# One query tile of 128 rows for the later chunk of two heads, in three attentions of a two-layer encoder

## The chip, the cores and the metric

The kernel runs on one core of a Trainium2 chip. The metric is the device time of one execution in microseconds (us); lower is better. TensorE (PE in the profile) multiplies matrices, VectorE (DVE), ScalarE (ACT) and GpSimd (POOL) work on tiles elementwise, SyncE (SP) issues the DMA transfers. Each engine works through its own list of instructions in order and waits for the others by semaphores.

## The reference, cut to what matters

Two layers of an encoder run over 1024 frames of a first chunk group ("prompt") and over 64 frames of a later chunk ("sample"), which have 256 cached keys and their own 64. Layer 0 has two groups of 8 heads, latent attention (A) and band attention (B), layer 1 has 16 heads of stick-breaking attention (C). Head size is 64. Around them stand projections, an output projection, layer norms and an MLP with 4096 hidden features.

```python
def _softmax_attend(q, k, v, mask, scale):               # A
    s = jnp.einsum('bqhd,bkhd->bhqk', q, k).astype(jnp.float32) * scale
    p = jax.nn.softmax(jnp.where(mask, s, NEG_INF), axis=-1)
    return jnp.einsum('bhqk,bkhd->bqhd', p.astype(v.dtype), v)

def _band_sample(q, k_all, v_all, n_past, table):        # B, later chunk
    ...
    s = jnp.einsum('bqhd,bkhd->bhqk', q, k_all).astype(jnp.float32) * BAND_SCALE + bias[None]
    p = jax.nn.softmax(s, axis=-1)
    return jnp.einsum('bhqk,bkhd->bqhd', p.astype(v_all.dtype), v_all)

def _stick_breaking(q, k, v, q_pos, k_pos):              # C
    z = jnp.einsum('bqhd,bkhd->bhqk', q, k).astype(jnp.float32) * SB_SCALE
    mask = k_pos[None, :] < q_pos[:, None]
    log_1m = jnp.where(mask, jax.nn.log_sigmoid(-z), 0.0)
    tail = lax.cumsum(log_1m, axis=z.ndim - 1, reverse=True) - log_1m
    w = jnp.where(mask, jnp.exp(jax.nn.log_sigmoid(z) + tail), 0.0)
    return jnp.einsum('bhqk,bkhd->bqhd', w.astype(v.dtype), v)
```

## The kernel before, in words

**Numbers.** Everything is fp32. [...]

**Heads.** Heads go in pairs: 4 in B, then 4 in A, then 8 in C. `heads64` (L444, for B and C) makes a pair's tiles: `qH` and `qL` (128 x 2 x 1088: both heads' queries of all 1088 rows, the half that belongs to the other part filled so that one K of 128 holds a product of two parts), `kS` (the keys) and `V` (128 x 11 x 2 x 128: 11 blocks of 128 keys, the last of which has only the 64 own keys of the later chunk; the value's high and low parts lie beside each other in the columns). In A a pair's queries come by DMA into `q` (128 x 2 x 1088), one tile per head, and the keys are `k0H` and the like. Two sets of tiles take turns by the pair's parity.

**Units.** `attend` (L649) walks `self.order`, a list of (head, unit). Units 0 to 3 are two blocks of 128 queries of the first group, unit 4 is the 64 later queries, a unit of its own for each head. A unit makes its rows of weights (`row_band`, `row_mla`, `row_stick`: scores on TensorE at L522 and L523, or by `mm3` in A; then softmax, or the scan and the product of C, on DVE, ACT and POOL into the tiles `R`, `Rs` or `G`), and `weigh` (L590) then transposes the weights block by block on TensorE (L161, into the PSUM tile `t`), splits them into `wtH` and `wtL`, and multiplies them with `V` into `pv` (L634, L635). For a late unit the scores have 64 query columns as the stationary operand, the transposes have 64 rows (two of 64 x 128 and one of 64 x 64), and the value matmuls of block 10 have 64 rows on both sides:

```python
            wH = self.tl(cp, [P, 512], "wtH", 3, F32R)
            ...
                nc.tensor.matmul(out, v, wH[:nkey, s : s + n], start=first, stop=False)
                nc.tensor.matmul(out, v, wL[:nkey, s : s + n], start=False, stop=last)
```

Then the two halves of `pv` are added: ACT copies the lower half to `otmp` (L637), DVE adds (L643); in A (`pool_fold`) ACT copies both (L637, L640) and POOL adds (L641). SP stores `o` (3 buffers) into `oT_d`, or `oTl_d` for the last pair of A and of C (L646).

**Order.** A scheduler with a simulated timeline fixes the order on each engine. `paced` (L507) ties each projection step of the next pair to the mark (first transpose) of a unit of the running one, so that the projections (L143 to L145, tile `d`) lie among the attention's matmuls. With the last pair of A and of C, the first output projections (`out_early`) take this place; behind it, `out_proj` (L949) loads `oTl_d` and `oT_d` in tiles `sl` and `xs`.

Of the kernel before, what the change touches and what calls it, by code (L numbers as in the profile page):

```python
# [7 lines left out]
F32 = mybir.dt.float32  # L8
# [5 lines left out]
P = 128  # L14
# [95 lines left out]
class Net:  # L110
# [3 lines left out]
    def __init__(self, tc, io):  # L114
        self.tc, self.nc, self.io = tc, tc.nc, io
        self.uid = 0
        self.alt = False
        self.wturn = 0
        self.pool_fold = False
# [324 lines left out]
    def heads64(self, cp, bp, qp, bufs, pair, w, cacheT, cache_v, outs, out0, cache_outs=(None, None), first=None):  # L444
# [16 lines left out]
        def step(kind, c0, n):  # L461
# [17 lines left out]
            if kind == "q":  # L479
                for h in range(2):  # L480
                    r, c = half[h], slice(c0, c0 + n)
                    self.split(qH[r, h, c], qL[r, h, c], ps[r, :n])
                    nc.scalar.activation(qH[half[1 - h], h, c], ps[r, :n], AF.Copy)
                return mark
# [17 lines left out]
        heads = []  # L502
        for h in range(2):
            heads.append(([qH[:, h, :], qL[:, h, :]], [kS[:, h, :]]))
        return heads, V, steps

# [11 lines left out]
    def scores(self, qk, qc, nq, kc, n, tag="s"):  # L518
        ps = self.ps(tag)
        q, k = ([x[:, c : c + m] for x in y] for y, c, m in zip(qk, (qc, kc), (nq, n)))  # L520
        if len(k) == 1:
            self.nc.tensor.matmul(ps[:nq, :n], q[0], k[0], start=True, stop=False)  # L522
            self.nc.tensor.matmul(ps[:nq, :n], q[1], k[0], start=False, stop=True)  # L523
        else:
            self.mm3(ps[:nq, :n], *q, *k)
        return ps

    def softmax_tail(self, rp, R, nq, nk, sums):
        nc = self.nc
        inv = self.tl(rp, [P, 1], "inv", 4)  # L530
        nc.vector.reciprocal(inv[:nq], sums)  # L531
        nc.gpsimd.tensor_tensor(R[:nq, :nk], R[:nq, :nk], inv[:nq].to_broadcast([nq, nk]), op=ALU.mult)  # L532

    def row_band(self, rp, qk, bias, qc, nq, kc, nk, off):
# [4 lines left out]
        for i, (a, n) in enumerate(pcs):  # L539
            ps = self.scores(qk, qc, nq, kc + a, n)  # L540
            nc.vector.tensor_tensor_reduce(
                R[:nq, a : a + n], ps[:nq, :n], bias[:nq, off + a : off + a + n], op0=ALU.add, op1=ALU.max, scale=1.0,
                scalar=-3e38 if i == 0 else mx[:nq, 0:1], accum_out=mx[:nq, i : i + 1])
        nm = self.tl(rp, [P, 1], "nm", 4)
        nc.vector.tensor_scalar(nm[:nq], mx[:nq, len(pcs) - 1 : len(pcs)], -SCALE, None, op0=ALU.mult)
        sm = self.tl(rp, [P, 1], "sm", 4)
        nc.scalar.activation(R[:nq, :nk], R[:nq, :nk], AF.Exp, bias=nm[:nq], scale=SCALE, accum_out=sm[:nq])
        self.softmax_tail(rp, R, nq, nk, sm[:nq])
        return [(0, nk, R)]

    def row_mla(self, rp, qk, qc, nq, kc, nk):
# [4 lines left out]
        for i, (a, n) in enumerate(pcs):  # L556
            ps = self.scores(qk, qc, nq, kc + a, n, tag="ds")
            nc.vector.tensor_tensor_reduce(
                R[:nq, a : a + n], ps[:nq, :n], self.zero[:nq].to_broadcast([nq, n]), op0=ALU.add, op1=ALU.max, scale=1.0,
                scalar=-3e38 if i == 0 else mx[:nq, 0:1], accum_out=mx[:nq, i : i + 1])  # L560
        nc.vector.tensor_scalar(nm[:nq, 0:1], mx[:nq, len(pcs) - 1 : len(pcs)], -MLA_SCALE, None, op0=ALU.mult)
        nc.scalar.activation(R[:nq, :nk], R[:nq, :nk], AF.Exp, bias=nm[:nq, 0:1], scale=MLA_SCALE, accum_out=sm[:nq, 0:1])
        self.softmax_tail(rp, R, nq, nk, sm[:nq, 0:1])
        return [(0, nk, R)]

    def row_stick(self, rp, qk, qc, nq, kc, nk):
# [1025 lines left out]
```

## Time and profile before

| | us |
|---|---|
| runs timed | 2878.89, 2874.23, 2879.42; median 2878.89 |
| profiled execution | 2872.33 (its span 2870.5, mean TensorE clock 0.986) |
| busy PE | 2766.8 (96% of the span, 16955 instructions) |
| busy DVE | 2165.0 (75%) |
| busy ACT | 1525.1 (53%) |
| busy POOL | 795.9 (28%) |
| chain of waits that ended last | PE 77%, DVE 9%, DMA 6%, ACT 3% |

The span falls into stages: latents up to 140 us, attention B 140 to 410, loads and query projections for A 410 to 497, A 497 to 690, output projection and MLP 690 to 1480, C 1480 to 2080 (its last pair from 1995 on), output projection and MLP to the end. In a timeline row of TensorE the second number is the modelled duration, which overlaps with the next; what a matmul costs is read from start to start.

### The profile page before, as it was taken

The page shows a single profiled execution, that of the slowest core. Times are in us where ns is not written, and L with a number is a line of the kernel's source. Part 1 is how long each engine was busy: PE and PEld are TensorE (multiplying, and loading weights), DVE is VectorE, ACT ScalarE, POOL GpSimd, SP SyncE. Part 2 cuts the span into 40 slices and gives each one's busy share as a digit, 9 for nine tenths or more (in the row PEclk, how much of TensorE's full clock was granted, in tenths as well). Part 3 has the DMA queues.
Part 4 walks back from the last instruction along what each step waited for, and adds up shares of the span by engine and source line. Part 5 has one row for each costly group of instructions (what it writes and reads, how often), then busy time and mean ns, then how long its engine had stood idle before and what let it go on. Part 6 is the DMA issues. An engine that isn't in the chain of part 4 may idle for free.

```text
span 2870.5 us, 47260 instructions
## 1 busy us (share of the span) xinstructions
PE 2766.8 (96%) x16955; PEld 2512.4 (88%) x16955; DVE 2165.0 (75%) x3905; ACT 1525.1 (53%) x3156; POOL 795.9 (28%) x900
## 2 busy tenths in 40 slices
PE   7999988999999999999999999999999999999998
PEld 7999977887899998888789999998779999977786
DVE  4256674785877777899987888888677777789998
ACT  4266653883455555433247777777444555553331
POOL 2123340662300002222533444444330000122235
PEclk9999999999999999999999999999899999999999
DMA  7222246334334447444231111112142344654432
GB/s 228 59 65 58 58 134 166 83 96 124 114 113 159 138 147 256 140 156 129 88 111 54 51 58 54 51 50 100 49 162 100 128 161 135 211 188 140 158 119 77
DMA packets 232041, 334.96 MB, mean 117 GB/s; under 512 B 43296, under 2 KB 165440, under 8 KB 230784
## 3 DMA queue, kind: packets, MB, share of 16 engines
q1 hardware_dynamic: 231808, 331.95, 36.5%
q8 instruction: 134, 2.20, 0.3%
q14 instruction: 99, 0.81, 0.1%
HBM read 217.18 MB, written 113.33 MB: 115 GB/s over the span
## 4 chain that ended last, share of the span: by engine, by line
PE 77%; DVE 9%; DMA 6%; ACT 3%; issue 3%; POOL 1%; SPq 1%; DVEq 0%; ACTq 0%; POOLq 0%
PE d L143 9%; PE d L145 9%; PE d L144 9%; PE s L143 5%; PE s L145 5%; PE s L144 5%; PE t L143 5%; PE t L145 5%; PE t L144 5%; PE t L161 5%; PE pv L634 3%; PE pv L635 2%; PE pv L145 2%; PE pv L143 2%; PE pv L144 2%
## 5 line engine op out<-in xcount | busy, mean ns | idle before, releaser
L585 POOL TENSOR_TENSOR G<-G,S 128x384 f32<-128x384 f32 (+4 forms) x208 | 210.3, 1013 | 330.5 <-DVE S L582 139.4
L143 PE MATMUL d<-xH,wH 128*128 128x384 f32 (+1 forms) x792 | 265.6, 335 | 3.7 <-ACT kraw L493 3.5
L145 PE MATMUL d<-xH,wL 128*128 128x384 f32 (+1 forms) x792 | 264.0, 333 | 1.6 <-DVE wL L139 1.6
L144 PE MATMUL d<-xL,wH 128*128 128x384 f32 (+1 forms) x792 | 263.9, 333 | 0.0
L139 DVE TENSOR_TENSOR wtL<-t,wtH 128x512 fp32r<-128x512 f32 (+4 forms) x376 | 200.8, 556 | 45.4 <-ACT wtH L138 42.7
L138 ACT ACTIVATE wtH<-t 128x512 fp32r<-128x512 f32 (+4 forms) x376 | 175.9, 497 | 75.1 <-PE t L161 42.1
L634 PE MATMUL pv<-wtH,V 128*128 128x256 f32 (+3 forms) x720 | 189.4, 285 | 11.7 <-DVE o L643 4.2
L532 POOL TENSOR_TENSOR R<-R,inv 128x640 f32<-128x640 f32 (+6 forms) x104 | 125.3, 1215 | 252.0 <-DVE inv L531 114.2
L635 PE MATMUL pv<-wtL,V 128*128 128x256 f32 (+3 forms) x720 | 183.6, 292 | 5.3 <-DVE wtL L139 5.3
L582 DVE TENSOR_TENSOR_SCAN S<-S,own 128x129 f32<-128x129 f32 (+2 forms) x144 | 150.0, 1047 | 20.0 <-ACT S L576 18.1
L634 PEld LDWEIGHTS pv<-wtH,V 128*128 128x128 f32 (+1 forms) x720 | 140.8, 196 | 27.2 <-ACT o L640 6.7
L143 PEld LDWEIGHTS d<-xH,wH 128*128 128x128 f32 x792 | 149.3, 189 | 7.7 <-ACT kraw L493 5.5
L145 PEld LDWEIGHTS d<-xH,wL 128*128 128x128 f32 x792 | 149.2, 188 | 3.5 <-DVE wL L139 1.9
L144 PEld LDWEIGHTS d<-xL,wH 128*128 128x128 f32 x792 | 149.4, 189 | 2.1
L635 PEld LDWEIGHTS pv<-wtL,V 128*128 128x128 f32 (+1 forms) x720 | 140.8, 196 | 9.1 <-DVE wtL L139 7.7
L138 ACT ACTIVATE wo<-wo 128x1024 fp32r<-128x1024 f32 (+4 forms) x100 | 88.0, 883 | 111.7 <-DMA wo<-a_d 20.3
L522 PE MATMUL s<-kS,qH 128*128 128x384 f32 (+4 forms) x312 | 114.8, 370 | 9.6 <-ACT G L577 6.2
L161 PE MATMUL t<-ident,G 128*128 128x128 f32 (+2 forms) x624 | 111.4, 279 | 6.0 <-POOL S L574 4.4
L576 ACT ACTIVATE S<-s 128x384 f32<-128x384 f32 (+4 forms) x208 | 101.8, 490 | 17.7 <-PE s L523 15.8
L523 PE MATMUL s<-kS,qL 128*128 128x384 f32 (+4 forms) x312 | 105.0, 338 | 0.0
L139 DVE TENSOR_TENSOR wo<-wo,wo 128x1024 fp32r<-128x1024 f32 (+3 forms) x72 | 83.8, 1164 | 26.4 <-ACT wo L138 26.3
L577 ACT ACTIVATE G<-s 128x384 f32<-128x384 f32 (+4 forms) x208 | 102.2, 492 | 0.8 <-PE t L161 0.8
(1702 smaller groups left out, 9778.2 us busy)
## 6 DMA issues: line engine op xcount, KB each, us to landing
wo<-a_d SPq DMA_DIRECT2D x53, 512.0 KB, 5.1
a_d<-wo SPq DMA_DIRECT2D x34, 544.0 KB, 4.4
sl<-a_d SPq DMA_DIRECT2D x29, 512.0 KB, 3.5
wo<-in_w_up SPq DMA_DIRECT2D x26, 512.0 KB, 3.9
wo<-in_w_dn SPq DMA_DIRECT2D x25, 512.0 KB, 5.9
sl<-in_w_dn SPq DMA_DIRECT2D x23, 512.0 KB, 4.9
xs<-a_d SPq DMA_DIRECT2D x19, 512.0 KB
a_d<-sl SPq DMA_DIRECT2D x17, 544.0 KB, 3.8
```

The source lines that it names most:

```text
L138: self.nc.scalar.activation(H, src, AF.Copy)
L139: (engine or self.nc.vector).tensor_tensor(L, src, H.bitcast(F32), op=ALU.subtract)
L143: i = mm(out, aH, bH, start=first, stop=False)
L144: mm(out, aH, bL, start=False, stop=False)
L145: mm(out, aL, bH, start=False, stop=last)
L161: return self.nc.tensor.transpose(out, in_, self.ident[:n, :n])
L522: self.nc.tensor.matmul(ps[:nq, :n], q[0], k[0], start=True, stop=False)
L532: nc.gpsimd.tensor_tensor(R[:nq, :nk], R[:nq, :nk], inv[:nq].to_broadcast([nq, nk]), op=ALU.mult)
L582: nc.vector.tensor_tensor_scan(s, s, own, carry, op0=ALU.mult, op1=ALU.max)
L585: nc.gpsimd.tensor_tensor(G[:nq, :n], G[:nq, :n], S[:nq, 1 : n + 1], op=ALU.mult)
L634: nc.tensor.matmul(out, v, wH[:nkey, s : s + n], start=first, stop=False)
L635: nc.tensor.matmul(out, v, wL[:nkey, s : s + n], start=False, stop=last)
```

## The change

The later queries of both heads of a pair become one unit of 128 rows. `self.order` has 9 entries instead of 10; (0, 4) now stands for both heads, and the last (1, 4) is gone. The queries stand in a tile `qS`, head 0 in columns 0 to 63 and head 1 in 64 to 127, zeros elsewhere, so that two accumulated products (one per head) give the 128 rows of scores. The last block of keys is filled up: rows 64 to 127 of `V`'s block 10 are zeroed once, and `pad` zeroes the last 64 columns of the weights. `set64` makes one set of tiles per parity for a whole attention, with the zeros written once, where `heads64` made tiles and zeros for each pair. In A, `q` holds only the first group's queries and `qS` is zeroed by POOL and loaded by 4 small DMAs per pair. In B the biases of both late heads are loaded into `blate`. `weigh` is left with full blocks, and `weigh_late` is new; `otmp` is used in A alone, elsewhere ACT copies into `o` and DVE adds there.

```diff
-        self.order = [(0, 3), (1, 0), (0, 2), (1, 1), (0, 4), (1, 3), (0, 0), (1, 2), (0, 1), (1, 4)]
+        self.order = [(0, 3), (1, 0), (0, 2), (1, 1), (0, 4), (1, 3), (0, 0), (1, 2), (0, 1)]
...
+    def set64(self, qp):
+        qH, qL = (self.tl(qp, [P, 2, SEQ], f"q{x}", 1, F32R) for x in "HL")
+        qS = self.tl(qp, [P, 2, 2, P], "qS", 1, F32R)
...
+        for h in range(2):
+            zero(qL[half[1 - h], h, :])
+        zero(qS)
+        zero(V[DEC:, 10])
...
+                    if m < n:
+                        c = slice(h * DEC, h * DEC + DEC)
+                        self.split(qS[r, h, 0, c], qS[r, h, 1, c], ps[r, m:n])
+                        nc.scalar.activation(qS[half[1 - h], h, 0, c], ps[r, m:n], AF.Copy)
...
+    def pad(self, R, nk):
+        n = -(-nk // P) * P
+        if n > nk:
+            self.nc.gpsimd.memset(R[:, nk:n], 0.0)
+        return n
...
+    def turn_weights(self, cp, blocks):
+        tp = self.ps("t")
+        mark = None
+        for i, (x, c) in enumerate(blocks):
+            t = self.transpose(tp[:, i * P : i * P + P], x[:, c : c + P])
...
+    def put_output(self, cp, pv, width):
+        nc = self.nc
+        o = self.tl(cp, [64, 256], "o", 3)
+        if self.pool_fold:
+            tmp = self.tl(self.pool_fold, [64, 256], "otmp", 2)
...
+        else:
+            nc.scalar.activation(o[:, :width], pv[64:128, :width], AF.Copy)
+            nc.vector.tensor_tensor(o[:, :width], pv[:64, :width], o[:, :width], op=ALU.add)
...
+    def weigh_late(self, cp, R, heads):
+        mm = self.nc.tensor.matmul
+        pv = self.ps("pv", (P, 256))
+        wH, wL, mark = self.turn_weights(cp, [(R[0][2], j * P) for j in range(3)])
+        for h, (V, hh, _) in enumerate(heads):
+            out = pv[:, h * DEC : h * DEC + DEC]
+            for j in range(3):
+                s = slice(j * P + h * DEC, j * P + h * DEC + DEC)
+                mm(out, V[:, 8 + j, hh, :], wH[:, s], start=j == 0, stop=False)
+                mm(out, V[:, 8 + j, hh, :], wL[:, s], start=False, stop=j == 2)
+        o = self.put_output(cp, pv, P)
...
+            qS = self.tl(mp, [P, 2, 2, P], "qS", 2, F32R)
+            nc.gpsimd.memset(qS.bitcast(F32), 0.0)
```

The order on TensorE in attention C, one late unit: `s` are scores, `t` transposes, `d` projections of the next pair, `pv` the outputs. Before, head 0 of a pair:

```order
L523 MATMUL s_18112<-kS_17742,qL_17741 128x512
L161 MATMUL t_17716<-ident_58,G_17706 64x64
L145 MATMUL d_18699<-xH_3484_16259,wL_4001_18689 128x384
...
L145 MATMUL d_18731<-xH_3483_16258,wL_4001_18689 128x384
L634 MATMUL pv_17715<-wtH_17718,V_16804 128x64
L635 MATMUL pv_17715<-wtL_17719,V_16804 128x64
L634 MATMUL pv_17715<-wtH_17727,V_16804 128x64
L635 MATMUL pv_17715<-wtL_17728,V_16804 128x64
```

and with the change (a pair):

```order
L542 MATMUL s_18143<-kS_16550,qL_16548 128x512
L161 MATMUL t_18079<-ident_58,G_18065 128x128 x3
L674 MATMUL pv_18021<-wtH_18027,V_16551 128x256
...
L143 MATMUL d_18549<-xH_3306_16007,wH_3782_18482 128x320
L691 MATMUL pv_18078<-wtH_18083,V_16551 128x64
L692 MATMUL pv_18078<-wtL_18084,V_16551 128x64
...
L692 MATMUL pv_18078<-wtL_18084,V_16551 128x64
L542 MATMUL s_18173<-kS_16550,qH_16547 128x512
```

The transpose of 64 x 64 and the two value matmuls on the 64-row block are gone; three transposes of 128 x 128 stand together, and the value matmuls, six per head, lie in one run without a block of its own shape in it.

The order on GpSimd where attention A begins: `R` and `Rs` are weights that it scales by `inv`. Before:

```order
L532 TENSOR_TENSOR R_5894<-R_5894,inv_5910 128x1024
L532 TENSOR_TENSOR Rs_5971<-Rs_5971,inv_5982 128x128
L532 TENSOR_TENSOR Rs_5985<-Rs_5985,inv_5996 128x256
L532 TENSOR_TENSOR R_6018<-R_6018,inv_6034 128x640
L532 TENSOR_TENSOR R_6037<-R_6037,inv_6053 128x768
```

and with the change:

```order
L880 MEMSET qS_5700 128x512
L880 MEMSET qS_6368 128x512
L549 TENSOR_TENSOR R_5745<-R_5745,inv_5761 128x896
L549 TENSOR_TENSOR R_5764<-R_5764,inv_5780 128x1024
L880 MEMSET qS_7036 128x512
L549 TENSOR_TENSOR Rs_5841<-Rs_5841,inv_5852 128x128
L549 TENSOR_TENSOR Rs_5855<-Rs_5855,inv_5866 128x256
```

Two of the memsets of `qS` stand ahead of the first scalings, the third (for pair 2, into pair 0's buffer) behind two of them, where it needs pair 0's late scores to be done.

The order on SyncE at the end of attention A: stores of `o` into `oTl_d`, and loads of the output projection (`wo`, `sl`, `xs`; `wraw` and `wH` are the layer norm's rows). Before:

```order
L646 DMA oTl_d<-o_8517 64x256
L932 DMA wo_19_2308_8809<-in_x 128x1024
L963 DMA sl_4_2344_8907<-oTl_d 128x128
L646 DMA oTl_d<-o_8577 64x256
L962 DMA sl_4_2408_9218<-oT_d 128x7x128
L963 DMA sl_4_2408_9218<-oTl_d 128x128
L646 DMA oTl_d<-o_8617 64x64
L962 DMA xs_0_2356_8950<-oT_d 128x7x128
```

and with the change:

```order
L679 DMA oTl_d<-o_8220 64x256
L1013 DMA wo_19_2130_8557<-in_x 128x1024
L679 DMA oTl_d<-o_8303 64x256
L679 DMA oTl_d<-o_8363 64x256
L1044 DMA sl_4_2166_8655<-oTl_d 128x128
L290 DMA wraw_8651<-in_ln_mix_g 128x1024
L290 DMA wH_2165_8653<-in_ln_mix_b 128x1024
```

The last store is one of a full unit (64 x 256) instead of 64 x 64, and the loads `sl` of `oTl_d` that stood ahead of the last two stores now follow all of them.

## Rows read from the trace of the kernel before

**Rows 1.** Stage stretches: stretch us, busy us (instructions) per engine, PEclk, DMA share, GB/s.
```profile
140.00:410.00 270.00, 259.62 (x1702) 247.73 (x1700) 186.91 (x579) 175.92 (x416) 104.40 (x104) 0.99 0.27 80
497.00:690.00 193.00, 182.08 (x1144) 160.27 (x1145) 144.82 (x483) 143.05 (x351) 106.43 (x112) 0.96 0.32 82
1480.00:1995.00 515.00, 503.78 (x3336) 481.63 (x3335) 415.03 (x622) 374.04 (x895) 208.53 (x390) 1.00 0.18 56
1995.00:2080.00 85.00, 72.89 (x364) 60.18 (x363) 60.54 (x79) 45.84 (x97) 32.92 (x45) 0.84 0.29 93
```

**Rows 2.** Groups by line and shape: value matmuls on a 64-row block of keys.
```profile
L634 PE MATMUL pv<-wtH,V 64*128 64x64 f32 x32 | 9.4, 294 | 0.0
```

**Rows 3.** Timeline, TensorE: start us, us, instruction; one transpose of 64x64.
```profile
1552.48 0.30 PE L145 MATMUL d<-xH,wL 128*128 128x320 f32 x1
1552.72 0.24 PE L161 MATMUL t<-ident,G 64*64 64x64 f32 x1
...
1553.14 0.31 PE L144 MATMUL d<-xL,wH 128*128 128x320 f32 x1
```

**Rows 4.** Timeline, TensorE: two transposes of 64 rows.
```profile
333.20 0.31 PE L145 MATMUL d<-xH,wL 128*128 128x320 f32 x1
333.44 0.33 PE L161 MATMUL t<-ident,R 64*128 64x64 f32 x2
...
333.96 0.31 PE L144 MATMUL d<-xL,wH 128*128 128x320 f32 x1
```

**Rows 5.** Timeline, TensorE: value matmuls of a 64-row block, then of full blocks.
```profile
1693.00 0.31 PE L143 MATMUL d<-xH,wH 128*128 128x320 f32 x1
1693.24 0.29 PE L634 MATMUL pv<-wtH,V 64*128 64x64 f32 x1
...
1693.58 0.30 PE L634 MATMUL pv<-wtH,V 128*128 128x64 f32 x1
1693.71 0.28 PE L635 MATMUL pv<-wtL,V 128*128 128x64 f32 x1
1693.82 0.28 PE L634 MATMUL pv<-wtH,V 128*128 128x64 f32 x1
```

**Rows 6.** Timeline, TensorE: three transposes of 128 rows.
```profile
1708.85 0.34 PE L144 MATMUL d<-xL,wH 128*128 128x384 f32 x1
1709.03 0.49 PE L161 MATMUL t<-ident,G 128*128 128x128 f32 x3
...
1709.53 0.33 PE L143 MATMUL d<-xH,wH 128*128 128x384 f32 x1
```

**Rows 7.** Timeline, TensorE: a late score with 64 stationary columns, then a projection.
```profile
1707.66 0.31 PE L523 MATMUL s<-kS,qL 128*64 128x320 f32 x1
1707.81 0.34 PE L144 MATMUL d<-xL,wH 128*128 128x384 f32 x1
```

**Rows 8.** Timeline, TensorE: last value matmul and first held matmuls, attentions A, C.
```profile
689.03 0.28 PE L635 MATMUL pv<-wtL,V 128*128 128x64 f32 x1
...
696.10 0.50 PE L143 MATMUL s<-wH,xs 128*128 128x512 f32 x1 [0.78 <-ACT xs L138]
...
697.90 0.50 PE L143 MATMUL s<-wo,xs 128*128 128x512 f32 x1 [0.60 <-ACT xs L138]
...
2081.57 0.28 PE L635 MATMUL pv<-wtL,V 128*128 128x64 f32 x1
...
2086.62 0.39 PE L145 MATMUL d<-wo,wo 128*128 128x512 f32 x1
2089.63 0.80 PE L143 MATMUL s<-wo,sl 128*128 128x512 f32 x1 [2.63 <-ACT sl L138]
```

**Rows 9.** Timelines, TensorE and GpSimd: first late score and first scalings of attention A.
```profile
503.48 0.31 PE L143 MATMUL d<-k0H,q 128*64 128x320 f32 x1
506.10 0.97 POOL L532 TENSOR_TENSOR Rs<-Rs,inv 128x128 f32<-128x128 f32 x2
```

**Rows 10.** Groups by line and shape, ScalarE: the copy into o in attention A.
```profile
L640 ACT ACTIVATE o<-pv 64x256 f32<-64x256 f32 x32 | 12.1, 377 | 1.6 <-DMA oT_d<-o 0.8
```

More of the change, by code (lines that the diff above doesn't have):

```diff
@@ L625, in weigh @@
-            wH = self.tl(cp, [P, 512], "wtH", 3, F32R)
-            wL = self.tl(cp, [P, 512], "wtL", 3, F32R)
-            self.split(wH[:nkey, :slot], wL[:nkey, :slot], tp[:nkey, :slot])
-            for (j, qs), s in zip(bank, place):
-                n = nq * len(qs)
-                out = pv[:, qs[0] * nq : qs[0] * nq + n]
-                v = V[:nkey, j, hh, :]
-                first = bi == 0 and s == 0
-                last = bi == len(banks) - 1 and j == bank[-1][0]
-                nc.tensor.matmul(out, v, wH[:nkey, s : s + n], start=first, stop=False)
-                nc.tensor.matmul(out, v, wL[:nkey, s : s + n], start=False, stop=last)
@@ L645, in weigh @@
-        dst = self.oTl_d if blk == self.late else self.oT_d[blk - (blk > self.late)]
-        nc.sync.dma_start(dst[r : r + 64, c0 : c0 + width], o[:, :width])
+                    blocks += [(x, c - p0) for p0, pn, x in R if p0 <= c < p0 + pn]
+            wH, wL, m = self.turn_weights(cp, blocks)
+            mark = mark or m
+            s = 0
+            for j, qs in bank:
+                n = P * len(qs)
+                out = pv[:, qs[0] * P : qs[0] * P + n]
+                v = V[:, j, hh, :]
+                mm(out, v, wH[:, s : s + n], start=bi == 0 and s == 0, stop=False)
+                s += n
+                mm(out, v, wL[:, s - n : s], start=False, stop=bi == len(banks) - 1 and j == bank[-1][0])
@@ L773, in rotate, with row @@
             return first
-        qk, V, steps = proj(0, first)
+        score, V, steps = proj(0, first)
         self.paced(steps, None)
         for pair in range(4):
-            heads = [((qk[h], bias_tile(2 * pair + h)), V, h, 512 + (2 * pair + h) * 64) for h in range(2)]
+            heads = [(V, h, 512 + (2 * pair + h) * 64) for h in range(2)]
+            bias = [bias_tile(2 * pair + h) for h in range(2)] + [bias_late(pair)]
+            def row(h, i, kc, nk):
+                return self.row_band(bp, score(h, i), bias[2] if i == 8 else bias[h][:, 640 - nk :], kc, nk)
             if pair == 3:
@@ L840, in even_mixer @@
                     p.release()
[L841 removed]
+            marks = self.attend(cp, heads, row, 0)
             if pair == 3:
```

249 lines of the change are left out of this document (130 added, 119 removed).

## The prediction

> **What bounds the kernel now.** I read the page first: PE is busy 96% of the span and holds 77% of the chain of waits, DVE 75%, ACT 53%. Then the busy time by stage, since an average over stages hides which of them has slack. In the three attentions [rows 1] PE is busy 259.62 of 270 us in B (96%), 182.08 of 193 in A (94%), and 503.78 + 72.89 of 515 + 85 in C (96%). DVE, the next in line (the third column of counts, behind TensorE's weight loads), has 186.91 of 270 (69%), 144.82 of 193 (75%) and 415.03 of 515 (81%). So in all three the time is TensorE's, and what the change is worth is read from its starts. Since the modelled durations overlap, I price a group of matmuls by what it adds from the start of the matmul ahead of it to the start of the second one behind it, less what the two neighbours take by themselves. The second one behind counts, because a change of shape delays the first one behind, too.
>
> **What leaves TensorE.** The count hardly changes: per pair the transposes go from 6 to 3, while 12 value matmuls and the late scores (4 in B and C, 6 in A) stay. What goes are the shapes of 64 rows. The group of value matmuls on a 64-row block appears 32 times at L634 [rows 2], once per late head: 16 pairs of two heads. Per late head:
> - one transpose of 64x64: 1552.48 to 1553.14 is 0.66 [rows 3], less two projections of 320 columns at 0.15 (1692.85 to 1693.00 [rows 5]): 0.36;
> - two transposes of 64 rows: 333.20 to 333.96 is 0.76 [rows 4], less 0.30: 0.46;
> - the value matmuls L634 and L635 of the 64-row block: 1693.00 to 1693.71 is 0.71 [rows 5], less 0.15 for the projection and 0.11 (1693.71 to 1693.82) for the first full one behind: 0.45.
>
> Two heads: 2 x (0.36 + 0.46 + 0.45) = 2.54 us per pair. **What comes in their place:** three transposes of 128 rows, 1708.85 to 1709.53 or 0.68 [rows 6], less two projections of 384 columns, at 0.18 (1708.85 to 1709.03): 0.32; and two pairs of full value matmuls at 0.24 (1693.58 to 1693.82 [rows 5]): 0.48. That is 0.80, so a pair saves 1.74 us: 7.0 in B, 7.0 in A, 13.9 in C, 27.9 in all. TensorE is not busy all the time, so I take the busy share of each stage of it: 7.0 x 0.96 + 7.0 x 0.94 + 13.9 x 0.96 = **26.6 us**. Bounds: the full 27.9 and more if the switches cost more elsewhere than in the places I read, and 0 if they are no price of the shape (rival 2).
>
> **The late scores** have 128 stationary columns instead of 64. The next start behind one of 64 columns and 320 moving ones comes 0.15 later [rows 7], as behind a projection with 128 columns [rows 5]: cost 0.
>
> [...]
>
> [...]
>
> **The hand-overs.** At the end of A and C the last unit is now a full one, and the output projection's loads follow its store. In A, 26 matmuls stood between the last value matmul and the first held one (689.03 to 696.10 [rows 8]). At 0.23 each (2081.57 to 2086.62 [rows 8] is 5.05 for 22 starts) that is 6.0 us of cover for 7.07 us of store, load and split; the idle time put down to it was 0.78. In the new order 14 matmuls, 3.2 us, stand there, then 6 that already need a load of `oTl_d` (`sl`), which was issued ahead of the last two stores and is now behind them. So the same chain of 7.07 has between 4.6 us of cover (20 matmuls), 1.4 less than before, and 3.2, 2.8 less. Bounds: 0, if the shorter load of `sl` is quicker than the old chain by that much, and 3.5, if it also delays what comes behind; I take **+2.0**, between 1.4 and 2.8. In C 22 matmuls covered 5.05 of 8.06 us (2081.57 to 2089.63), and 2.63 were waited [rows 8]. Now 40 matmuls, 9.2 us, stand there: the wait goes, **−2.6** (at worst 0).
>
> **GpSimd.** In A `qS` is zeroed per pair. Its duration is not in the trace; the nearest rows are the scalings of 128x128, 0.97 for two [rows 9], so 0.5, between 0 and 2. The memset for pair 2 waits for pair 0's late scores; the first of these started at 503.48, while POOL came to its first scalings only at 506.10 [rows 9], so it is ready, and what queues behind it (scalings, and on SP the loads of `qS` and the stores) loses only the 0.5: **+0.5**, since A begins with PE waiting for those weights. Of four memsets the other three lie in POOL's idle time (106.43 of 193 busy [rows 1]).
>
> **Free edits.** The projection step at the end of the queries writes its last 64 columns apart: four more ACT and two more DVE instructions per pair in B and C. At 0.38 each (the copy of 64x256 [rows 10], which is longer) that is 1.5 us on ACT per pair, against 94 us idle in B (270 − 175.92 [rows 1]): covered; were the cover gone, up to 18 us over 12 pairs. The late units give ACT, DVE and POOL half as many passes, the zeros for `qL` are written 8 times instead of 24, and 16 stores of `oTl_d` and `oT_d` go: nothing gained, as TensorE hides them. Padding adds a memset of 64 columns per late unit on POOL, cheaper than the scaling it saves.
>
> **Sum:** −26.6 + 2.0 − 2.6 + 0.5 = −26.7. Against the profiled execution's 2872.33 that is 2845.6. The median of the runs shown, 2878.89, is 6.6 above that execution; a median of the changed kernel then comes to **2852**. From here "no change" means within 0.2%, 5.8 us, about what a measurement of this kernel tells apart.
>
> **Rivals.**
> 1. *The other engines set the pace in A and B.* With TensorE shorter, the chain of scores, softmax, scaling and split becomes the bound there, and only C's 13.3 us are realised. For it: PE is idle 4% of B and 6% of A already. Against it: DVE is busy only 69% and 75% there, and the late units' passes on it are halved. 2878.9 − 13.3 + 2.0 − 2.6 + 0.5 = 2865.5, say 2866.
> 2. *The change does not do what it is written to do:* the excess around the 64-row groups is their neighbours' (a wait on `t` or `wtH`), not the shape's. Then only three transposes fewer per pair count, at 0.107 (0.32 / 3 [rows 6]): 16 x 0.32 x 0.96 = 4.9, less 0.1: 2874, no change. Against it: the rows show no wait at these groups, and the same excess at three shapes.
> 3. *Slower: a new wait on `o`.* In B and C, ACT now writes `o` straight from `pv`, and must wait until the store from that buffer, three folds back, has landed; before, it wrote `otmp`, which only DVE reads. `pv` has one buffer, so PE's next value matmuls stand behind that copy. A has this already: ACT idles 0.8 us for a store over 32 folds [rows 10], 0.025 each. B and C have 12 x 9 = 108 folds; at that price 2.7 us of ACT, mostly hidden. It decides from (26.7 + 5.8) / 108 = 0.3 us per fold, when SP lags by two units, since it works its queue in order and stores stand behind loads that wait. At 0.33: 36 us, 2852 + 36 = 2888.
>
> **How the numbers follow.** The forecast 0.70 (its own range 2842 to 2863), rival 1 0.16, rival 2 0.08, rival 3 0.06. The range 2838 to 2870: the low end is the full 27.9 (1.3 lower), the hand-over in A at 0 (2.0), POOL's memset at 0 (0.5), 5.5 if the groups of 64 rows cost a fifth more on the mean than where I read them, and 4.7 if the median lies as low among its runs as the 2874.23 did before; the high end takes in rival 1 with A's hand-over at 3.5 and POOL's memset at 2. Left out are rivals 2 and 3 and what lies below. Faster 0.86 (forecast and rival 1), no change 0.08, slower 0.06.
>
> **What would show it.** In the changed trace no TensorE group in an attention has 64*64 or 64*128, transposes of 128*128 alone come in threes, and the starts behind them keep 0.11 per transpose. B ends about 7 us earlier, A another 7 less 2, C 13 or 14. At the end of C no wait near 2.63 stands at the first matmul with `sl`; at the end of A a wait of 1 to 4 us does. ACT's copies into `o` show idle time for a DMA of `oT_d` under 5 us in all; much over 20 would be rival 3. If B and A do not shorten while DVE's or POOL's releases stand ahead of PE's matmuls, it is rival 1; if the pitches around the new groups keep the excess, rival 2.

## The result, and the profile after

The change takes 1.1% off: 2845.79 us median (2842.44 to 2849.38) against 2877.27 of the kernel before in the same comparison, ratio 0.9892 (95% interval 0.9877 to 0.9907), which is 31.5 us, between 26.8 and 35.4. The time lies in the forecast range, and the kernel got faster, as forecast; the forecast gain was 26.7 us. The profiled execution took 2842.44 (span 2840.6), 29.9 us less.

The page of the changed kernel, busy time of each engine:

```profile
PE 2737.7 (96%) x16907; PEld 2499.6 (88%) x16907; DVE 2160.4 (76%) x3837; ACT 1512.2 (53%) x3104; POOL 776.0 (27%) x890
```

TensorE's share stays 96%: 29 us of busy time went and 30 us of span. Its groups by line and shape, of the transposes and the late value matmuls:

```profile
L161 PE MATMUL t<-ident,G 128*128 128x128 f32 x600 | 107.4, 282 | 12.6 <-POOL G L610 6.4 <-POOL S L598 2.9 <-DVE wtL L139 2.5
L692 PE MATMUL pv<-wtL,V 128*128 128x64 f32 x96 | 22.2, 276 | 0.0
L691 PE MATMUL pv<-wtH,V 128*128 128x64 f32 x96 | 21.3, 266 | 0.6 <-ACT o L634 0.6
```

No group of 64 rows is left in an attention; the group of [rows 2] is gone, and the late value matmuls are 96 + 96 of full shape. The timeline of TensorE shows their price, and that of the transposes in front of them:

```profile
212.33 0.34 PE L145 MATMUL d<-xH,wL 128*128 128x384 f32 x1
212.51 0.19 PE L691 MATMUL pv<-wtH,V 128*128 128x64 f32 x1
...
213.65 0.28 PE L692 MATMUL pv<-wtL,V 128*128 128x64 f32 x1
213.76 0.44 PE L161 MATMUL t<-ident,R 128*128 128x128 f32 x2
...
1726.90 0.83 PE L542 MATMUL s<-kS,qS 128*128 128x320 f32 x4
1727.57 0.27 PE L161 MATMUL t<-ident,G 128*128 128x128 f32 x1
```

Twelve value matmuls take 1.25 us (212.51 to 213.76), 0.21 a pair where the forecast had 0.24. Four late scores with 128 stationary columns take 0.67 us or 0.17 each (1726.90 to 1727.57), near the 0.15 of 64 columns in [rows 7].

Where the time went is a matter of places, so I measured each stage of both timelines from the first to the last value matmul (`pv<-wt`) of an attention; for B from its first score.

| stretch, us | before | after | difference |
|---|---|---|---|
| up to B's first score | 166.5 | 167.9 | +1.3 |
| B | 279.2 | 260.5 | −18.7 |
| B's end to A's first value matmul | 62.3 | 62.3 | 0 |
| A | 181.0 | 171.1 | −9.9 |
| A's end to C's first value matmul | 836.5 | 842.3 | +5.8 |
| C | 556.1 | 544.9 | −11.1 |
| C's end to the last matmul | 778.5 | 781.2 | +2.7 |

(The differences are of unrounded times, each from one profiled execution.) C's is flattered: 18 more matmuls stand behind its last value matmul, 4.1 us at 0.23, and lie in the last row instead. Measured to the first matmul with `sl` behind it, C has lost 9.8 us. The forecast had 6.7 for B, 6.6 less 2.0 for A and its hand-over, and 15.9 for C and its own: the sum fits, the places do not. B has nearly three times its share, A gains more and gives more back (4.1 net, of 4.6), C has two thirds. Three questions follow: are the shapes what pays, what else moved in B, and what is missing in C?

The windows of the changed kernel on these stretches, and three of 5 us that are used below (stretch us, busy us (instructions) of PE, PEld, DVE, ACT, POOL, then PEclk, DMA share, GB/s):

```profile
167.90:428.30 260.40, 245.16 (x1653) 238.51 (x1653) 187.71 (x566) 170.29 (x402) 94.66 (x99) 0.98 0.30 89
490.60:661.80 171.20, 163.27 (x1083) 147.61 (x1083) 131.07 (x416) 130.63 (x303) 96.98 (x104) 0.99 0.34 88
670.00:675.00 5.00, 0.98 (x2) 0.83 (x3) 3.48 (x7) 2.51 (x3) 1.66 (x2) 0.79 1.12 338
675.00:680.00 5.00, 5.00 (x14) 3.71 (x13) 3.90 (x4) 2.02 (x3) 1.28 (x1) 0.53 0.97 316
1504.00:2048.90 544.90, 520.42 (x3392) 492.61 (x3391) 450.43 (x636) 388.47 (x915) 216.79 (x396) 0.97 0.18 58
1594.00:1599.00 5.00, 5.00 (x23) 5.00 (x23) 4.29 (x7) 3.50 (x9) 2.65 (x3) 0.66 0.15 46
```

### The profile page after: what moved, and what is told of

It is laid out like the page before. It is cut to its first block, busy times and chain, and to the rows that moved or that the text cites. A ratio compares the mean times of both kernels' runs of the same rounds, so it can differ in the third digit from the quotient of the medians.

```text
span 2840.6 us, 46995 instructions
## 1 busy us (share of the span) xinstructions
PE 2737.7 (96%) x16907; PEld 2499.6 (88%) x16907; DVE 2160.4 (76%) x3837; ACT 1512.2 (53%) x3104; POOL 776.0 (27%) x890
## 4 chain that ended last, share of the span: by engine, by line
PE 78%; DVE 9%; ACT 4%; DMA 4%; issue 3%; POOL 1%; SPq 0%; DVEq 0%; ACTq 0%; POOLq 0%
PE d L143 9%; PE d L144 9%; PE d L145 9%; PE s L143 5%; PE s L145 5%; PE s L144 5%; PE t L143 5%; PE t L144 5%; PE t L145 5%; PE t L161 4%; PE s L542 3%; PE pv L676 2%; PE pv L674 2%; PE pv L145 2%; PE pv L143 2%
## 5 line engine op out<-in xcount | busy, mean ns | idle before, releaser
L139 DVE TENSOR_TENSOR wtL<-t,wtH 128x512 fp32r<-128x512 f32 (+2 forms) x328 | 196.8, 618 | 54.3 <-ACT wtH L138 47.1
L138 ACT ACTIVATE wtH<-t 128x512 fp32r<-128x512 f32 (+2 forms) x328 | 170.6, 545 | 64.4 <-PE t L161 32.8
L674 PE MATMUL pv<-wtH,V 128*128 128x256 f32 (+1 forms) x624 | 159.3, 280 | 8.3 <-ACT o L634 4.0
L676 PE MATMUL pv<-wtL,V 128*128 128x256 f32 (+1 forms) x624 | 155.2, 289 | 7.0 <-DVE wtL L139 7.0
L607 DVE TENSOR_TENSOR_SCAN S<-S,own 128x513 f32<-128x513 f32 (+3 forms) x144 | 143.9, 1006 | 13.8 <-ACT S L600 12.2
L138 ACT ACTIVATE wo<-wo 128x1024 fp32r<-128x1024 f32 (+4 forms) x100 | 87.9, 883 | 113.9 <-DMA wo<-a_d 21.4
L674 PEld LDWEIGHTS pv<-wtH,V 128*128 128x128 f32 x624 | 120.1, 192 | 13.7 <-ACT o L634 6.3
L676 PEld LDWEIGHTS pv<-wtL,V 128*128 128x128 f32 x624 | 120.0, 192 | 10.8 <-DVE wtL L139 9.6
L161 PE MATMUL t<-ident,G 128*128 128x128 f32 x600 | 107.4, 282 | 12.6 <-POOL G L610 6.4
L542 PE MATMUL s<-kS,qH 128*128 128x384 f32 (+3 forms) x288 | 106.4, 372 | 4.9 <-ACT G L601 2.7
L139 DVE TENSOR_TENSOR wo<-wo,wo 128x1024 fp32r<-128x1024 f32 (+3 forms) x72 | 81.9, 1140 | 24.2 <-ACT wo L138 24.2
L542 PE MATMUL s<-kS,qL 128*128 128x384 f32 (+3 forms) x288 | 97.7, 341 | 0.0
```

The costliest lines, as they stand in the source:

```text
L138: self.nc.scalar.activation(H, src, AF.Copy)
L139: (engine or self.nc.vector).tensor_tensor(L, src, H.bitcast(F32), op=ALU.subtract)
L161: return self.nc.tensor.transpose(out, in_, self.ident[:n, :n])
L542: self.nc.tensor.matmul(ps[:, :n], q, k, start=i == 0, stop=i == len(passes) - 1)
L607: nc.vector.tensor_tensor_scan(s[r], s[r], own, carry, op0=ALU.mult, op1=ALU.max)
L674: mm(out, v, wH[:, s : s + n], start=bi == 0 and s == 0, stop=False)
```

## The experiments

Theory 1: the shapes of 64 rows are what pays, in each attention as forecast. Theory 2: what pays is who is late at the ends of the stages, since the order of units and loads has moved; in the middle of a stage other waits take the place of what the shapes give back.

**One attention at a time.** The first kernel keeps the old code for B and A and takes the changed one in C; the second the other way round.

```diff
 # e1_c_only: odd_mixer and what it calls from the changed kernel, the rest from before
 # e2_ab_only: even_mixer and what it calls from the changed kernel, the rest from before
```

> The change in attention C alone, B and A as before. Theory 1 (the 64-row shapes: 1.74 us per pair, wherever they stand) expects 8 x 1.74 x 0.96 = 13 us and the wait of 2.6 at the end of C: about 16 us less than before, near 2861, with the middle of C shorter by 1.5 us or more per pair. Theory 2 (what counts is who is late at the ends of the stages; in the middle of C other waits take the place of what the shapes give back) expects only what the trace of the changed kernel shows behind the last value matmuls of C, 8 to 9 us: near 2868, with the middle of C as long as before.

> The change in attentions B and A alone, C as before. Theory 1 expects 8 x 1.74 x 0.95 = 13 us, less the longer hand-over at the end of A (waits of 7 us instead of 1.4): about 8 us less than before, near 2869. Theory 2 expects the 20 us that the trace shows at the end of B (loads of w_uq come earlier, PE waits 6 us less for them) and nearly nothing net in A: 20 to 23 us less, near 2856.

Measured: C alone 0.9962 (0.9949 to 0.9974) or 10.9 us; B and A alone 0.9926 (0.9914 to 0.9939) or 21.3. The two add up to 32.2, about the 31 of the whole change. In the stretches, C alone has B at 278.8, A at 180.0 and C at 545.6; B and A alone have 263.0, 171.4 and 554.6. So each stage's difference is its own, and it repeats within 3 us. As a whole the numbers lie with theory 2 for B and A, and for C between the two.

**The order without the shapes.**

```diff
-        self.order = [(0, 3), (1, 0), (0, 2), (1, 1), (0, 4), (1, 3), (0, 0), (1, 2), (0, 1), (1, 4)]
+        self.order = [(0, 3), (1, 0), (0, 2), (1, 1), (0, 4), (1, 4), (1, 3), (0, 0), (1, 2), (0, 1)]
...
-        self.order = [(0, 0), (1, 3), (0, 1), (1, 2), (0, 4), (1, 0), (0, 3), (1, 1), (0, 2), (1, 4)]
+        self.order = [(0, 0), (1, 3), (0, 1), (1, 2), (0, 4), (1, 4), (1, 0), (0, 3), (1, 1), (0, 2)]
```

> The kernel before with its late units moved only: (1, 4) stands right behind (0, 4), so that the last unit of a pair is a full one as in the change, and all shapes, tiles and counts stay. Theory 1 expects no gain in the pairs, a hand-over in A that is longer by 5 us, and one in C that is shorter by 2.6: 0 to 3 us slower than before. Theory 2 expects the early loads at the end of B (8 to 14 us) and the end of C (up to 8 us), less 5 in A: 10 to 17 us less than before.

Measured: 0.9975 (0.9966 to 0.9984), 7 us less than before, between the two expectations. B is 270.6 (8.6 shorter, with every 64-row shape in it), A 180.1 and C 555.1 (each 0.9 shorter): theory 2 holds in B and falls in C. The stretch behind A is 838.1, 1.6 longer than before: the forecast's +2.0 for a full unit at A's end is about what the order alone costs there.

What moved in B is a load. In the kernel before, the timelines of SyncE, ScalarE and TensorE at the end of B:

```profile
417.21 0.59 SPq L751 DMA_DIRECT2D raw<-in_rope_feat  x1
...
422.44 0.91 SPq L169 DMA_DIRECT2D wraw<-in_w_uq  x1
...
431.49 0.84 ACT L138 ACTIVATE wH<-wraw 128x768 fp32r<-128x768 f32 x1 [12.55 <-DMA wraw<-in_w_uq]
...
434.65 0.63 PE L143 MATMUL d<-qnH,wH 128*128 128x320 f32 x1 [5.98 <-DVE raw L139]
```

The load of `w_uq` (`wraw`) for the first projection behind the rotated parts stands in SP's list behind a load of `raw` that went out at 417.21 only, and itself goes out at 422.44. ScalarE waits 12.55 us for it (3.5 until it goes out, 9.0 until its copy starts) with the rest of its list behind it, the copies of `raw` that free PSUM too, and TensorE waits 5.98. In the changed kernel, SyncE and TensorE:

```profile
401.22 0.58 SPq L802 DMA_DIRECT2D raw<-in_rope_feat  x1
403.72 0.36 SPq L169 DMA_DIRECT2D wraw<-in_w_uq  x1
...
425.03 0.44 PE L143 MATMUL d<-qnH,wH 128*128 128x384 f32 x1 [2.00 <-DVE raw L139]
```

The load goes out at 403.72, ScalarE's list has no such wait, and TensorE's is 2.00. In the run with the order alone the load goes out at 414.90, and TensorE waits 2.05 at that place. The late unit no longer closes the pair, and the scheduler lets the loads ahead. No run moves this load alone, so that its part of the 8.6 us is read from these waits.

**The shapes without the order.** The shared unit with 64-row shapes put back:

```diff
-        wH, wL, mark = self.turn_weights(cp, [(R[0][2], j * P) for j in range(3)])
+        for h, (V, hh, _) in enumerate(heads):
+            tp = self.ps("t")
+            r = slice(h * DEC, h * DEC + DEC)
+            for j in range(3):
+                n = P if j < 2 else DEC
+                t = self.nc.tensor.transpose(tp[:n, j * DEC : j * DEC + DEC], R[0][2][r, j * P : j * P + n], self.ident[r, r])
...
+            for j in (2, 0, 1):
+                n = P if j < 2 else DEC
+                mm(out, V[:n, 8 + j, hh, :], wH[:n, s], start=j == 2, stop=False)
```

> The changed kernel with the 64-row shapes put back: in the shared late unit each head's weights are transposed by themselves (two of 64 x 128 and one of 64 x 64) and block 10 is multiplied on 64 rows; scores, order and everything else stay shared. Theory 1 expects to lose what the shapes cost, 26 us, back to 2872. Theory 2 expects to lose it in B and A at most (13 us), and nothing in the middle of C: 2850 to 2860.

Measured: 0.9969 (0.9956 to 0.9981). Against the changed kernel's 0.9892 the shapes (with the splits by head that come along) cost 0.77% or 22.2 us, some 5 either way by the two intervals, of the 26.6 forecast: theory 1 for the whole. By stretch: B 267.4 (7.0 more than the changed kernel; forecast 6.7), A 179.6 (8.4; 6.6), C 551.5 (6.6; 13.3). By stretch, A and B cost what was forecast or more, C half. In A this is not the shapes alone: TensorE's idle time is 2.8 us longer than in the changed kernel, and 5 more matmuls (1.2 us) lie ahead of its last value matmul. C's half is taken up again below.

**The hand-over in A.** In the changed kernel, the timelines of TensorE and ScalarE:

```profile
666.81 0.51 PE L143 MATMUL s<-wo,sl 128*128 128x512 f32 x1 [1.52 <-ACT sl L138]
674.01 0.79 PE L143 MATMUL s<-wH,xs 128*128 128x512 f32 x1 [5.53 <-ACT xs L138]
...
666.45 0.31 ACT L138 ACTIVATE sl<-sl 128x128 fp32r<-128x128 f32 x1 [3.53 <-DMA sl<-oTl_d]
671.30 1.15 ACT L268 ACTIVATE wo<-wo,neg 128x1024 f32<-128x1024 f32 x1 [4.54 <-DVE neg L267]
672.91 1.06 ACT L138 ACTIVATE xs<-xs 128x1024 fp32r<-128x1024 f32 x1 [0.46 <-DMA xs<-oTl_d]
```

1.52 + 5.53 us are waited where [rows 8] had 0.78 and 0.60 for `xs`. ScalarE's copy for an early tile's layer norm (`wo`) stands ahead of the split of `xs` (L138 writes the high part on ScalarE, L139 subtracts it for the low part), but it is not what the split waits for: behind the copy, ScalarE still waits 0.46 for the load of `xs`. That load took long. The timelines of SyncE and ScalarE before, then of SyncE with the change:

```profile
691.46 0.56 SPq L963 DMA_DIRECT2D xs<-oTl_d  x1
...
693.75 0.41 SPq L290 DMA_DIRECT2D wraw<-in_ln_mix_g  x1
...
694.99 1.06 ACT L138 ACTIVATE xs<-xs 128x1024 fp32r<-128x1024 f32 x1 [5.13 <-DMA xs<-oTl_d]
```

```profile
665.13 0.33 SPq L290 DMA_DIRECT2D wraw<-in_ln_mix_g  x1
...
666.47 0.62 SPq L1044 DMA_DIRECT2D xs<-oTl_d  x1
```

From the issue of the load to the split it is 3.5 us before (691.46 to 694.99) and 6.4 with the change (666.47 to 672.91). The layer norm's rows (`wraw` and `wH`, both 128x1024) were issued behind that load before and are issued ahead of it now; the DMA share from 670 to 675 is 1.12. That these two loads hold up `xs` fits the order and the times, but no run moves them alone. Behind it TensorE's granted clock is lower: PEclk is 0.79 and 0.53 in the windows from 670 and 675, 0.50 in each us from 673 to 679. The repair:

```diff
+            if pair == 3:
+                self.order = [(0, 3), (1, 0), (0, 2), (1, 1), (1, 3), (0, 0), (1, 2), (0, 1), (0, 4)]
             marks = self.attend(cp, heads, row, 0)
```

> The changed kernel with the late unit put last in the order of A's fourth pair alone, so that the store that the output projection waits for is the small one again. Theory (the hand-over in A was mis-sized: two waits of 1.5 and 5.5 us because the loads follow a full unit): these waits fall to 1 to 2 us and the kernel gains about 5 us on the changed one, ratio to before near 0.987. Rival (the projection's operand is late anyway, because ScalarE works through its queue behind a layer norm): no gain, ratio as that of the change, 0.989.

Measured: 0.9882 (0.9870 to 0.9895), whose interval holds the change's own 0.9892. In the timelines of that kernel:

```profile
673.85 0.50 PE L143 MATMUL s<-wH,xs 128*128 128x512 f32 x1 [1.96 <-ACT xs L138]
...
672.74 1.06 ACT L138 ACTIVATE xs<-xs 128x1024 fp32r<-128x1024 f32 x1 [2.56 <-DMA xs<-oTl_d]
```

The wait fell to 1.96. The load of `xs` goes out at 668.89, ahead of the layer norm's rows (670.44 and 670.92), and the split starts 3.9 us later. The stretch from A's end to C's first value matmul is 839.2 instead of 842.3, but A itself is 172.5 instead of 171.1: 1.7 us of the forecast five are left, and on the total that is too little to be told apart in one comparison.

**Is C bound by TensorE?** A product by `mm3` is three matmuls of the operands' high and low parts (high by high, high by low, low by high). The second is left out in a part of C's query projections: 64 matmuls, full shapes, nothing else.

```diff
-                i = self.mm3(out, wH[:, k, :], wL[:, k, :], xH[:, k, c0 : c0 + n], xL[:, k, c0 : c0 + n], k == 0, k == nk - 1)
+                i = mm(out, wH[:, k, :], xH[:, k, c0 : c0 + n], start=k == 0, stop=False)
+                mm(out, wL[:, k, :], xH[:, k, c0 : c0 + n], start=False, stop=k == nk - 1)
```

> The kernel before with 64 matmuls left out in attention C (the high-by-low third of the query projections of the first 384 rows, 8 per pair, pitch 0.175): q there lacks one of its three products. 8 x 8 x 0.175 = 11.2 us of TensorE go, none of another engine, and no shape is mixed in. If C is bound by TensorE as its busy share says: 10.7 us less than before. If other engines hold C for a part (theory 2 in C): 4 to 7 us less.

> The changed kernel with the same 64 matmuls left out in attention C. If C is still bound by TensorE: 10.7 us less than the changed kernel (ratio to before 0.9855). If the change has brought C to where VectorE and ScalarE are late: 0 to 5 us less than the changed kernel (ratio 0.9875 to 0.989).

Both theories missed: the kernel before became slower, 1.0063 (1.0050 to 1.0077) or 18 us, and the changed one did not become faster (0.9909, 0.9897 to 0.9922, about 5 us above its own 0.9892, with intervals that overlap). The windows of e6_thin_before, most of C and three stretches of it:

```profile
1525.50:1990.00 464.50, 447.92 (x2854) 420.10 (x2853) 375.90 (x552) 336.26 (x802) 188.19 (x357) 0.96 0.16 50
1755.00:1760.00 5.00, 3.10 (x18) 2.27 (x16) 4.88 (x9) 3.95 (x12) 1.53 (x3) 0.88 0.35 107
1760.00:1765.00 5.00, 4.95 (x19) 3.95 (x19) 4.84 (x11) 4.89 (x14) 2.46 (x9) 0.50 0.24 72
1830.00:1835.00 5.00, 4.28 (x17) 3.81 (x18) 4.87 (x8) 4.71 (x14) 2.74 (x7) 0.55 0.17 51
```

and a wait ahead of the second and one in the third of them, in its TensorE timeline:

```profile
1758.44 0.57 PE L162 MATMUL t<-ident,G 128*128 128x128 f32 x3 [1.51 <-POOL G L591]
...
1830.50 0.48 PE L528 MATMUL s<-kS,qH 128*128 128x128 f32 x1 [0.89 <-ACT G L583]
```

The scheduler made another order out of the shorter lists, with waits of 0.9 to 1.5 us in the pairs; the granted clock is 0.50 in the window behind the first wait shown and 0.55 in the one around the second, and over that stretch of C it is 0.96, where the kernel before had 1.00 in [rows 1] up to 1995. Not every such wait is followed by this: in the changed kernel the clock stays at 1.00 in the 5 us behind one of 1.15 at 1659.82. So this run does not price TensorE's work in C; it shows that a new order of the lists by itself moves C by as much as is looked for here (13.3 us longer in e6_thin_before, with less to do).

**VectorE relieved?** Weights' low parts by GpSimd in C:

```diff
-        self.split(tiles[1], tiles[2], tiles[0])
+        self.split(tiles[1], tiles[2], tiles[0], self.nc.gpsimd if self.weight_pool else None)
```

> The changed kernel with the low part of C's weights (three subtractions of 128x1024 per pair, 1.1 to 1.2 us each on VectorE) computed by GpSimd, nothing else changed: VectorE loses 24 x 1.15 = 28 us in C. If VectorE holds C for a part: 4 to 8 us less than the changed kernel, ratio 0.986 to 0.988. If C is bound by TensorE, or GpSimd's own lists get late: no gain or a loss of some us.

Measured: 0.9911 (0.9898 to 0.9924): no gain; C is 549.8. The window over C, then the scans of one shape in the changed kernel and in this one:

```profile
1509.80:2059.50 549.70, 520.61 (x3391) 491.37 (x3390) 451.83 (x616) 385.97 (x911) 260.68 (x415) 0.98 0.19 58
...
L609 DVE TENSOR_TENSOR_SCAN S<-S,S 128x513 f32<-128x513 f32 x16 | 25.3, 1583 | 4.4 <-ACT S L600 2.0 <-issue 1.8
...
L610 DVE TENSOR_TENSOR_SCAN S<-S,S 128x513 f32<-128x513 f32 x16 | 31.7, 1983 | 3.3 <-ACT S L601 1.0 <-issue 0.9 <-POOL G L611 0.5
```

VectorE was not relieved: it is busy 451.83 us in C, 450.43 in the changed kernel. The subtractions left its list, but its scans, all shapes together, take 256.5 us instead of 225.9, with 60.4 us of subtractions more on GpSimd. So this run does not test whether VectorE holds C.

**One place in VectorE's list.** In the changed kernel the longest wait of C's middle is this, in the timelines of VectorE, ScalarE and TensorE:

```profile
1589.00 1.72 DVE L607 TENSOR_TENSOR_SCAN S<-S,own 64x321 f32<-64x321 f32 x2
1590.75 0.22 DVE L139 TENSOR_TENSOR kS<-d,kS 64x64 fp32r<-64x64 f32 x1
...
1592.63 0.69 DVE L139 TENSOR_TENSOR wtL<-t,wtH 128x512 fp32r<-128x512 f32 x1
...
1591.00 0.22 ACT L138 ACTIVATE kS<-d 64x64 fp32r<-64x64 f32 x1 [1.08 <-DVE kS L139]
1591.24 0.60 ACT L138 ACTIVATE wtH<-t 128x512 fp32r<-128x512 f32 x1
...
1593.47 0.52 PE L161 MATMUL t<-ident,G 128*128 128x128 f32 x3 [2.48 <-DVE wtL L139]
```

The shared unit has two scans of 64 rows, since the two heads' own keys end at different columns of the mask; they used to lie in two units and now stand back to back, 1.72 us. Behind them waits a subtraction of `kS`, for that ScalarE with the copy of `wtH`, behind it VectorE's `wtL`, and TensorE waits 2.48; PEclk is 0.66 in the 5 us from 1594, and 0.50 in the two of them from 1595. A second mask tile makes one scan of 128 rows; a control has only the 16-bit mask that gives it room.

```diff
-                for r, end in ((slice(0, P), 512),) if kc < SEQ else ((slice(0, DEC), 448), (slice(DEC, P), 512)):
-                    own = self.own[r, end - n : end + 1][:, ::-1]
-                    nc.vector.tensor_tensor_scan(s[r], s[r], own, carry, op0=ALU.mult, op1=ALU.max)
+                own = (self.own[:, 512 - n : 513] if kc < SEQ else self.own2)[:, ::-1]
+                nc.vector.tensor_tensor_scan(s, s, own, carry, op0=ALU.mult, op1=ALU.max)
...
+        self.own2 = self.tl(bp, [P, 321], "own2", 1, mybir.dt.bfloat16)
+        nc.gpsimd.tensor_copy(self.own2[:DEC], self.own[:DEC, 128:449])
+        nc.gpsimd.tensor_copy(self.own2[DEC:], self.own[DEC:, 192:513])
```

> Control for the next run: the changed kernel with the mask tile own of attention C in 16 bits instead of 32 (it holds zeros and ones), the same order on every engine. Expected by all theories: the time of the changed kernel, ratio to before 0.989, with the same waits in C (2.5 us near the start of pair 1, TensorE at half its clock for some us behind it).

> The changed kernel with one scan of 128 rows for C's late unit instead of two of 64 rows back to back (a second mask tile holds each half's own diagonal; both mask tiles in 16 bits to find room). VectorE loses 8 scans of 0.86 us, and the block of 1.72 us in its list becomes 0.86. If the half of C's gain that is missing went to VectorE (waits for wtL behind that block, and the half clock that follows a wait): 4 to 8 us less than the changed kernel, ratio 0.986 to 0.988. If C's time is set by the order that the scheduler happens to find: anything within 10 us of the changed kernel, either way, with waits elsewhere.

Measured: control 0.9883 (0.9867 to 0.9899), the change's time, with its wait (2.49 at 1596.43) and a C of 544.3. One scan: 0.9861 (0.9847 to 0.9875). The intervals overlap, but each of its four runs (2834.45 to 2839.93) is below each of the control's five (2840.51 to 2849.22), by 6 us in the medians. In the profiled executions C is 535.1, 9.2 us less than in the control. The scans of e10_own2, its window over C, and the control's:

```profile
L606 DVE TENSOR_TENSOR_SCAN S<-S,own 128x321 f32<-128x321 f32 x8 | 7.2, 903 | 0.1
...
1505.50:2040.60 535.10, 515.40 (x3401) 490.28 (x3400) 452.57 (x628) 387.60 (x914) 205.62 (x396) 0.98 0.19 60
1507.00:2051.30 544.30, 519.78 (x3392) 492.17 (x3391) 450.31 (x636) 389.17 (x915) 218.05 (x396) 0.97 0.19 58
```

Eight scans of 0.90 do what sixteen of 0.89 did. No wait over 1 us is left in C before 1964, in its last pair. The gain is not less work on VectorE, whose busy time over C is 452.57 against 450.31, since the other scans take longer (all scans of C 232.6 us against 225.5). What is less is TensorE's idle time, 535.10 − 515.40 = 19.7 against 24.5 us, and its clock is 0.98 against 0.97. The order also changed elsewhere with this edit (31 matmuls stand behind C's last value matmul, 40 in the control), so that the block's part of the 9 us is shown by its wait (2.48 and the clock behind it) and not beyond.

**Both repairs,** e10_own2 with the order of e5_a_last:

> The run before with A's late unit last in the fourth pair, as in e5_a_last: 2 to 3 us less than that run, if the two repairs add.

Measured: 2832.97 us, ratio 0.9847 (0.9829 to 0.9864), the fastest of the runs and faster than both kernels; the gain on e10_own2, 5 us in the medians where 2 to 3 were expected, lies inside the intervals.

**The shapes in C again,** with the single scan: e10_own2 with the 64-row shapes of e4_rows64.

> The single scan of e10_own2 together with the 64-row shapes of e4_rows64. If the shapes cost in C what the forecast had (13 us) once VectorE's block no longer takes part of it: C is 12 to 14 us longer here than in e10_own2, and the whole 22 to 27 us (ratio to before 0.994 to 0.9955). If the shapes are worth only half of that in C whatever VectorE does: C 5 to 8 us longer, the whole 17 to 20 us (ratio 0.992 to 0.993).

Measured: 0.9947 (0.9935 to 0.9959), 0.86% or 24.7 us more than e10_own2, some 5 either way by the two intervals. C is 548.8, 13.6 more; A is 179.7, 8.5 more; B 273.0, 11.5 more, with TensorE's clock at 0.94 there against 0.97. (The two profiled executions lie 32.8 us apart, more than the ratio says, so a stage's number is good to some us.) The first of the two expectations holds. The windows over C of e4_rows64 and of this run:

```profile
1520.00:2071.50 551.50, 531.34 (x3430) 496.63 (x3429) 457.48 (x660) 391.59 (x939) 215.15 (x396) 0.98 0.19 58
1528.40:2077.20 548.80, 529.08 (x3426) 495.77 (x3424) 449.20 (x652) 392.21 (x939) 217.06 (x396) 0.98 0.19 58
```

In this run TensorE is idle 548.80 − 529.08 = 19.7 us in C, as in e10_own2, at the same clock of 0.98, and 31 matmuls stand behind C's last value matmul in both. So the 13.6 us are TensorE's own time, with no more waiting, and near the forecast 13.3. The 6.6 of e4_rows64 was not such a pair: TensorE idles 20.2 us there and 24.5 in the changed kernel, the clock is 0.98 against 0.97, and 26 matmuls stand behind the last value matmul against 40, so that 14 more, 3.2 us, lie within C. An estimate from these numbers, 6.6 − 3.2 + 4.3 and some 5 for a hundredth of the clock, comes to 13 again: the shapes cost the same there, and the changed kernel pays part of it back in waits and clock.

## Why the prediction was right, and where not

- **The shapes (−26.6): right,** and measured twice, at 22.2 and 24.7 us, each some 5 either way. What TensorE does at a change of shape was not shown, only its price: in the kernel before, the next start behind the first projection after the 64x64 transpose of [rows 3] comes 0.25 us later (1552.89 to 1553.14), where it is 0.15 for one of 320 columns in [rows 5]. The price from start to start over a changed shape was sound where it can be compared at equal idle time: B 7.0 for 6.7, C 13.6 for 13.3; A's 8.4 and 8.5 for 6.6 hold waits as well. In the change as made, C realised less: the factor 0.96 for TensorE's busy share was the step that failed there. It takes the waits and the clock of C as they were, and the changed kernel has 24.5 us of idle time at 0.97 where e4_rows64 has 20.2 at 0.98. Rival 1 named this mechanism, but in B and A, where nothing of it is seen; it happened in C, where VectorE is busiest (81% in [rows 1]).
- **The hand-over in A (+2.0): right in kind, too small.** The stretch grew by 5.8. The forecast gave the chain of store, load and split its old length of 7.07 us and shortened only the cover on TensorE. With the order alone (e3_order) that comes out, 1.6. In the change the chain itself is longer: from the issue of the load of `xs` to the split 6.4 us instead of 3.5, with the layer norm's rows issued ahead of it.
- **The hand-over in C (−2.6): as forecast in the place;** the first matmul with `sl` shows no wait. The stretch up to the end is 2.7 longer; 4.1 for the 18 matmuls that lie in it now, less the wait of 2.6, are 1.5 of that, and no run here took the rest apart.
- **GpSimd (+0.5): right in its size, not shown as a cost.** The memset of `qS` takes 0.52, as the row below shows, and lies between scalings as its order said; from B's end to A's first value matmul it is 62.3 us before and after.
- **What was not in the sum:** the end of B, 8.6 us by the order alone. The forecast read SP's list at the end of A and GpSimd's at A's start, not SP's at the end of B, where a load that goes out late holds three engines (waits of 12.55 us on ScalarE, 7.30 on VectorE, 5.98 on TensorE). The stage rows did not point there: [rows 1] close B at 410, while its value matmuls go on to 445.7. Of B's 18.7, 7.0 go with the shapes and 8.6 with the order; some 3 are left unassigned.
- **Rival 2** (the excess is not the shape's) falls with e4_rows64 and e12_own2_rows64. **Rival 3** (a wait on `o`) did not come: of the 44.3 us that the copies into `o` in B and C wait, 42.6 are for TensorE.
- **The range's low end** takes 5.5 us for groups of 64 rows that cost a fifth more. That is a fifth of the saving of 27.9; a fifth of the groups' own 16 x 2.54 = 40.6 is 8.1. The result does not hang on it.

The timeline of GpSimd and the copy's group on ScalarE in the changed kernel:

```profile
486.84 1.90 POOL L549 TENSOR_TENSOR R<-R,inv 128x1024 f32<-128x1024 f32 x1 [0.58 <-DVE inv L548]
488.68 0.52 POOL L880 MEMSET qS<- 128x512 f32 x1
489.16 0.97 POOL L549 TENSOR_TENSOR Rs<-Rs,inv 128x128 f32<-128x128 f32 x2
...
L637 ACT ACTIVATE o<-pv 64x256 f32<-64x256 f32 x96 | 36.5, 381 | 44.3 <-PE pv L676 42.6
```

So the total was right partly by luck: 12 us more from B than forecast, 8.6 of them by the order and not in the sum, and some 3 more from A stand against some 4 too little for A's hand-over and some 6 too much from C and its own.

## What to carry to other kernels

Price a shape by start to start across it, neighbours included, and put it back in an otherwise changed kernel to see it: here 64-row transposes and value matmuls cost 22 to 25 us of 2877, in C with no idle time to show for it. When a unit moves in an order, read the lists of all queues at the end of every stage, not only where the unit's result is awaited; at the end of B the order, and with it a load that held ScalarE for 12.55 us, was worth as much as the shapes of a whole attention. When two small pieces of work are joined on one engine, look at what they become on the others: two scans of 64 rows back to back stood ahead of the longest wait in C's middle. And when work is moved off an engine, look at that engine's busy time afterwards: in e8_c_pool it did not fall.

## What was not expected of the hardware

Removing 64 matmuls from C made the kernel 18 us slower, with other waits (1.51 us at 1758.44). Around and behind waits of 0.9 to 2.5 us the granted clock was 0.50 to 0.66 in windows of 5 us, though TensorE is busy there (5.00 of 5.00 us in the window from 1594, at 0.66). The length of the wait alone does not tell: in C of the kernel before, which waited 0.9 at most up to 1995, the clock stood at 1.00, in e6_thin_before it is 0.55 around a wait of 0.89, and behind one of 1.15 in the changed kernel it stayed at 1.00.

VectorE's scans had no fixed price here: those of 128x513 on `S` alone took 1583 ns on the mean in the changed kernel and 1983 in e8_c_pool, where GpSimd had 24 subtractions of 128x1024 more. One scan of 128 rows took as long as one of 64 (0.90 and 0.89 us for 321 columns).
